# Eight modulation steps of the second layer, moved from the first layer's mixer to the end of its experts

## The chip, the cores and the metric

The kernel runs on one core of one Trainium2 chip, as one program. The metric is the device time of one execution, in microseconds (us). Four engines compute: TensorE (PE, with its weight loads listed as PEld), VectorE (DVE), ScalarE (ACT) and GpSimd (POOL). SyncE (SP) issues most transfers. Each engine works through its own instructions in order and waits at semaphores for the others.

## The reference, cut to what matters

The model is a backbone of two layers over 256 latent tokens and 256 context tokens of width 1024. Each layer is modulated by vectors that depend on the conditioning alone:

```python
for layer in range(DEPTH):
    m_lat = jnp.split((s_lat @ ada_w[layer] + ada_b[layer])[:, None, :], 6, axis=-1)
    m_ctx = jnp.split(s_ctx @ ada_w[layer] + ada_b[layer], 6, axis=-1)
    h = modulate(rms_norm(x, norm_mix_g[layer]), m_lat[0], m_lat[1])
    ...
    y, yc = token_mix(h @ w_in[layer], hc @ w_in[layer], ...)
    x = x + m_lat[2] * (y @ w_out[layer])
    h2 = modulate(rms_norm(x, norm_ffn_g[layer]), m_lat[3], m_lat[4])
    x = x + m_lat[5] * moe_ffn(h2, ...)   # 16 experts, two per token
```

The matrix `ada_w[layer]` has 1024 rows and 6144 columns in fp32, 24 MB for each layer. The kernel multiplies it with the two conditioning vectors. The last 2048 columns of the second layer (its chunks 4 and 5) are first used in that layer's mixture of experts.

## The kernel before, in words

**Stages.** Each layer has a mixer (the projection w_in in chunks, and four groups of attention, C, B, A, D), an output projection, the routing, and sixteen experts. A layer's weights pass through the on-chip memory once, in pieces of 1 MB.

**The stream of weights.** All weight loads are listed beforehand in `jobs`, in the order of their use. `pump` (line 127) takes the next job when a slot of 8 KB per partition is free and issues the load on SyncE; each load is kept behind the one before it. `next_w` hands the next loaded piece to the code and `done_w` gives its slot back. The first layer has three slots "a" that live through the whole kernel, and nine slots "b" that exist from the end of attention to the end of the experts. Jobs whose name begins with e or o (experts, output projection) may use every slot; the others (`in...`, `blk...`, `ada...`) only an "a" slot. A job that finds no slot it may use holds back all jobs behind it.

**The modulation.** Five groups of 2048 columns (two of layer 0, three of layer 1) are computed in forty steps by `ada_step` (line 307), eight steps to a group. A step takes one load of 1 MB and issues four matmuls of 32 columns by 512 rows, each on its own quarter of the array. The eighth step of a group also adds the bias (line 323), writes the rows to the DRAM tile `amd`, transposes them (line 330) and copies them to `modT` (line 333). In the kernel before, `Mixer.project` calls all forty steps in the first layer's mixer, between the products of the projection; `ADAN` says how many belong to each of the ten chunks of w_in.

**The order of instructions.** A scheduler orders each engine's instructions, by program order as priority and by when it takes them to be ready. `pinned` ties an instruction to the one traced before it on the same engine. The experts' matmuls are pinned, so TensorE runs them in the order of the code.

**The seam between the layers.** `Moe.experts` runs the first projection of expert e+1 (`first`, lines 1018 and 1023) ahead of the second projection of expert e (`second`, lines 1071 and 1077). `store` scales a result and scatters its rows to the DRAM tile `yd` with GpSimd (line 987). `overflow` (line 1136) follows the last expert: it loads the largest count of tokens on an expert (line 1140) and processes the tokens over capacity in a conditional (line 1141). The conditional is one unit to the scheduler, with work for all engines; here the count is under the capacity and it is passed over. Then the second layer begins: `combine` reads `yd` back (`yy`, on the same stream as the weights) and adds the rows to X (line 1220), `make_hT` normalises and transposes X (lines 406 to 436), and `split_w` (lines 456 and 458) splits the weights of the projection into two parts. The tiles of the second layer's beginning lie where the "b" slots and the experts' tiles were.

Of the kernel before, what the change touches and what calls it, by code (L numbers as in the profile page):

```python
# [44 lines left out]
GROUPS = ("C", "B", "A", "D")  # L45
CHUNKS = dict(A=("Aq", "Akv"), B=("Bq", "Bk", "Bv"), C=("Cq", "Ck", "Cv"), D=("Dq", "Dkv"))

ADAN = (0, 3, 5, 5, 4, 4, 5, 5, 4, 5)
CH = dict(Aq=0, Akv=256, Bq=512, Bk=768, Bv=1024, Cq=1280, Ck=1536, Cv=1792, Dq=2048, Dkv=2304)
YC = dict(A=0, B=2, C=4, D=6)  # L50

# [1 line left out]
def body(tc, a, dbg=None):  # L53
    nc = tc.nc
    ctx = ExitStack()
    V, S, G, PE = nc.vector, nc.scalar, nc.gpsimd, nc.tensor

    def pool(name, bufs=1, space=None, stack=None, side=None):
        kw = {} if space is None else dict(space=space)
        if side is not None:  # L60
            kw["side"] = side
        return (stack or ctx).enter_context(tc.tile_pool(name=name, bufs=bufs, reuse_waits="tile", **kw))
# [9 lines left out]
    def psum(tag):  # L72
        return ps.tile([128, 512], F32, name=tag, bufs=dict(mm=2, ada=1, tr=2, S=2, o=1)[tag])
# [20 lines left out]
    slots_free = []  # L94
# [7 lines left out]
    def add_ring(pl, tag, order):  # L102
        rings[tag] = pl
        for i in range(len(order)):
            pl.tile([128, 2048], F32, name=f"w{tag}{i}", bufs=1)
        slots_free.extend((tag, i) for i in order)
        pump()


    def add_tile(tag, t):  # L110
        fixed[tag, 0] = t
        slots_free.append((tag, 0))
        pump()

    def slot(x):
        return fixed[x] if x in fixed else rings[x[0]].tile([128, 2048], F32, name=f"w{x[0]}{x[1]}", bufs=1)

    def drop_ring(tag):
        assert all(x[0] != tag for x in used)
        slots_free[:] = [x for x in slots_free if x[0] != tag]  # L120


    def stream(out, in_):
        with tc.issue_after(state["dma"]) if state["dma"] is not None else nullcontext():
            state["dma"] = nc.sync.dma_start(out, in_).ins

    def pump():
        while slots_free and state["emit"] < len(jobs):
            nm, view, src = jobs[state["emit"]]
            xs = [y for y in slots_free if y[0] == "a" or nm[0] in "eo"]  # L130
            if not xs:
                break
            x = xs[0]
            slots_free.remove(x)
            t = slot(x)
            tv = t.rearrange("p (k n) -> p k n", n=view)
            stream(tv, src.rearrange("(k p) n -> p k n", p=128))
            issued.append((nm, x, tv))
            state["emit"] += 1

    def next_w(nm):
        if not issued:
            pump()
        n, tag, t = issued.pop(0)
        assert n == nm, (n, nm)
        used.append(tag)
        return t


    def done_w(n=1):  # L150
        for _ in range(n):
            slots_free.append(used.pop(0))
        pump()
# [3 lines left out]
    def jobs_ada(n):  # L157
        for _ in range(n):
            l, cg, k = ada_q.pop(0)
            jobs.append((f"ada{l}{cg}", 2048, a["ada_w"][l, 128 * k:128 * k + 128, 2048 * cg:2048 * cg + 2048]))  # L160
# [6 lines left out]
    order = [nm for g in GROUPS for nm in CHUNKS[g]]  # L167

    def job_in(l, nm):
        jobs.append((f"in{l}{nm}", 256, a["w_in"][l, :, CH[nm]:CH[nm] + 256]))  # L170

    for l in range(L):
        if l == 0:
            job_in(0, order[0])
            for j in range(4):
                for h in range(2):
                    c0 = 1024 * h + 256 * j
                    jobs.append((f"blk{j}", 256, a["ada_w"][0, :, c0:c0 + 256]))
        for i, nm in enumerate(order):
            if l or i:  # L180
                job_in(l, nm)
            if l == 0:
                jobs_ada(ADAN[i])
        for g in GROUPS:
            c0 = 128 * YC[g]
            jobs.append((f"out{l}{g}", 1024, a["w_out"][l, c0:c0 + 256]))

        for e in range(NE + 1):
            for hk in range(2):
                for nm in ("w_gate", "w_up"):  # L190
                    if e < NE:
                        jobs.append((f"e{l}", 512, a[nm][l, e, 512 * hk:512 * hk + 512]))
            for hk in range(2):
                if e:
                    jobs.append((f"e{l}", 1024, a["w_down"][l, e - 1, 256 * hk:256 * hk + 256]))


    pk = const.tile([128, PKN], F32, name="pk")
# [13 lines left out]
    sc, rwp = scr2[:, 0], scr2[:, 1]  # L212
# [91 lines left out]
    amd = dram.tile([32, 512], F32, name="amd")  # L304
    acur = {}

    def ada_step(scr):
        l, cg, k = ada_run.pop(0)
        if k == 0:
            acur["p"] = psum("ada")  # L310
            ab = acur["b"] = scr.tile([128, 512], F32, name="abr")
            G.memset(ab, 0.0)
            for s in range(2):
                nc.scalar.dma_start(ab[s:128:32], a["ada_b"][l, 2048 * cg:2048 * cg + 2048].rearrange("(c n) -> c n", c=4))
        pa, ab = acur["p"], acur["b"]
        w = next_w(f"ada{l}{cg}")
        for c in range(4):
            PE.matmul(pa[32 * c:32 * c + 32], lhsT=sc[:, k], rhs=w[:, 0, 512 * c:512 * c + 512],  # L318
                      start=k == 0, stop=k == 7)
        done_w()  # L320
        if k < 7:
            return
        V.tensor_add(ab, pa, ab)
        if cg:
            for s in range(2):
                r0 = ((l * 2 + cg - 1) * 2 + s) * 4
                nc.scalar.dma_start(amd[r0:r0 + 4], ab[s:128:32])
        pt = psum("tr").rearrange("p (q n) -> p q n", n=128)
        for q in range(4):
            PE.transpose(pt[:, q], ab[:, 128 * q:128 * q + 128], ident)  # L330
        c0, c1, d0 = ((0, 4, 0), (2, 4, 16), (0, 2, 24))[cg]
        for s in range(2):
            V.tensor_copy(modT[l][:, s, d0:d0 + 4 * (c1 - c0)].rearrange("p (c q) -> p c q", q=4),
                          pt[:, :, 32 * c0 + s:32 * c1:32].rearrange("p q c -> p c q"))
# [115 lines left out]
    def split_w(nm, pl, tag, bufs):  # L450
        w = next_w(nm)
        wp = []
        for q in range(4):
            x = pl.tile([128, 2, 2, 256], F32R, name=tag, bufs=bufs)
            r = w[:, 2 * q:2 * q + 2]
            S.activation(x[:, 0], r, AF.Copy)  # L456
            cnt["lo"] += 1
            (G if cnt["lo"] % 4 == 0 else V).tensor_sub(x[:, 1], r, x[:, 0].bitcast(F32))  # L458
            wp.append(x)
        done_w()  # L460
        return wp
# [55 lines left out]
    class Mixer:  # L517
# [7 lines left out]
        def project(self, nm, tiles, done):  # L525
            l = self.l
            begun = self.begun.pop(nm, None)
            if begun is None:
                with prefer(l, -70, 0):
                    wp = split_w(f"in{l}{nm}", self.ws, "ws", 5)  # L530
            n = ADAN[order.index(nm)] if l == 0 else 0
            for i, t in enumerate(tiles):
                if begun is None:
                    acc = psum_x("mm", l, 3)[:, 0:256]
                    products(acc, self.hT, wp, t, range(8))
                else:
                    acc = begun[t]
                self.flush()
                later = done(t, acc)
                if later is not None:  # L540
                    self.pending.append(later)
                for _ in range(n * (i + 1) // len(tiles) - n * i // len(tiles)):
                    ada_step(self.ada)
# [238 lines left out]
    class Moe:  # L782
        order = staticmethod(pinned)
# [674 lines left out]
    for l in range(L):  # L1458
# [50 lines left out]
        scr = pool(f"op{l}", stack=stR, side=P)  # L1509
# [5 lines left out]
        moe = (Moe if l < L - 1 else MoeOnChip)(l, tiles, pers, scr)  # L1515
# [5 lines left out]
        w = {k: next_w(f"out{l}{k}") for k in GROUPS[:-1]}  # L1521
# [3 lines left out]
        w = {g: next_w(f"out{l}{g}")}  # L1525
# [28 lines left out]
        with ExitStack() as stE:  # L1554
            moe.experts(pool(f"moee{l}", stack=stE, side=P))
            if l < L - 1:
                moe.overflow()
        drop_ring("c")
        drop_ring("b")
# [118 lines left out]
```

## Time and profile before

| | |
|---|---|
| time, median of 3 runs | 1228.39 us (1226.92 to 1229.65) |
| the profiled execution, its own time | 1229.94 us |
| its span in the profile | 1228.2 us |
| mean granted clock of TensorE | 0.963 |
| busy: TensorE, VectorE, ScalarE, GpSimd | 1122.8, 568.9, 417.5, 244.5 us |
| HBM read | 305.11 MB, 257 GB/s over the span |

Times in the rows are microseconds from the start of the span, or lengths in microseconds unless marked ns. L318 is line 318 of the kernel. Of a group or a piece of the timeline, "out<-in" names the tile written and the tile read, "x16" says that it stands for sixteen instructions, and the bracket at the end gives the idle time of the engine before it and what ended it. SPq, PEldq and the like are the sequencers of the engines: branches, register loads and semaphore instructions, and the issue of transfers. A matmul of fp32 appears as two records.

### The profile page before, as it was taken

The page shows a single profiled execution, that of the slowest core. Times are in us where ns is not written, and L with a number is a line of the kernel's source. Part 1 is how long each engine was busy: PE and PEld are TensorE (multiplying, and loading weights), DVE is VectorE, ACT ScalarE, POOL GpSimd, SP SyncE. Part 2 cuts the span into 40 slices and gives each one's busy share as a digit, 9 for nine tenths or more (in the row PEclk, how much of TensorE's full clock was granted, in tenths as well). Part 3 has the DMA queues.
Part 4 walks back from the last instruction along what each step waited for, and adds up shares of the span by engine and source line. Part 5 has one row for each costly group of instructions (what it writes and reads, how often), then busy time and mean ns, then how long its engine had stood idle before and what let it go on. Part 6 is the DMA issues. An engine that isn't in the chain of part 4 may idle for free. (4 is left out here: it accounts for less than half of the span.)

```text
span 1228.2 us, 21412 instructions
## 1 busy us (share of the span) xinstructions
PE 1122.8 (91%) x8495; PEld 653.6 (53%) x8495; DVE 568.9 (46%) x1544; ACT 417.5 (34%) x1003; POOL 244.5 (20%) x269
## 2 busy tenths in 40 slices
PE   4999999999999949999999993899999969999996
PEld 2677667676645424444444432888787533443432
DVE  4465666656433563232222216966775342333323
ACT  3345455446314311111111113675664221221212
POOL 1141221121111531122112113623231120000000
PEclk9899899999999969999999996998999989999999
DMA  9756455283570839999999957221424969999996
GB/s 305 240 185 241 173 172 194 101 292 140 204 279 18 325 125 314 377 383 381 375 367 379 378 219 265 78 70 35 129 70 161 355 260 393 393 394 394 394 394 244
DMA packets 134640, 313.00 MB, mean 255 GB/s; under 512 B 7212, under 2 KB 38448, under 8 KB 129408
## 3 DMA queue, kind: packets, MB, share of 16 engines
q1 hardware_dynamic: 127936, 294.19, 66.1%
q0 software_dynamic: 3840, 8.40, 2.1%
q10 hardware_dynamic: 2752, 8.91, 2.0%
q8 instruction: 71, 1.16, 0.4%
q14 instruction: 41, 0.34, 0.1%
HBM read 305.11 MB, written 10.55 MB: 257 GB/s over the span
## 5 line engine op out<-in xcount | busy, mean ns | idle before, releaser
L469 PE MATMUL mm<-ws,hT 128*128 128x256 f32 x1488 | 230.2, 296 | 3.6 <-DVE hT L508 1.8
L469 PEld LDWEIGHTS mm<-ws,hT 128*128 128x128 f32 x1488 | 201.0, 195 | 41.2 <-issue 25.1
L1018 PE MATMUL mm<-wb,xT 128*32 128x512 f32 x912 | 121.8, 622 | 0.0
L299 POOL TENSOR_TENSOR hss<-hss,mhalf 128x4 f32<-128x4 f32 (+2 forms) x56 | 67.6, 1210 | 184.9 <-DVE hss L298 176.5
L675 ACT ACTIVATE p<-S,nm 128x512 f32<-128x512 f32 (+1 forms) x120 | 73.7, 616 | 67.7 <-DVE nm L665 41.3
L665 DVE TENSOR_REDUCE nm<-S 128x1 f32<-128x512 f32 (+1 forms) x120 | 70.5, 596 | 25.8 <-PE S L640 21.8
L987 POOL DMA_INDIRECT yd<-y,idx x32 | 37.7, 1179 | 170.4 <-DVE y L1096 165.5
L769 PE MATMUL mm<-wa,t4k 128*128 128x512 f32 x144 | 70.8, 614 | 0.0
L1018 PE MATMUL mm<-wb,xTb 128*64 128x512 f32 x240 | 63.2, 596 | 0.8 <-DMA wb<-in_w_up_dram 0.8
L318 PE MATMUL ada<-wa,sc 128*32 128x512 f32 x320 | 63.1, 617 | 0.0
L1018 PEld LDWEIGHTS mm<-wb,xT 128*32 128x32 f32 x912 | 31.7, 114 | 55.6 <-issue 49.7
L1071 PE MATMUL S<-wb,hT 128*32 128x512 f32 (+1 forms) x360 | 56.1, 593 | 0.0
L648 PE MATMUL tr<-ident,p 128*128 128x128 f32 x320 | 51.0, 277 | 4.1 <-ACT p L675 3.5
L716 PE MATMUL o<-PT,v 128*64 128x256 f32 x320 | 54.5, 390 | 0.1
L456 ACT ACTIVATE ws<-wa 128x512 fp32r<-128x512 f32 x80 | 48.8, 630 | 16.9 <-PE mm L469 7.5
L458 POOL TENSOR_TENSOR ws<-wa,ws 128x512 fp32r<-128x512 f32 x20 | 27.9, 1395 | 133.3 <-ACT ws L456 108.5
L615 PE MATMUL tr<-identr,sk 128*128 128x128 f32 x312 | 47.5, 254 | 5.3 <-DVE sk L612 3.4
L1018 PE MATMUL mm<-wc,xTb 128*64 128x512 f32 x144 | 50.6, 596 | 0.0
L1057 ACT ACTIVATE hT<-tr 128x384 f32<-128x384 f32 (+1 forms) x32 | 14.0, 438 | 105.6 <-PE tr L1054 68.2
L648 PEld LDWEIGHTS tr<-ident,p 128*128 128x128 f32 x320 | 36.5, 140 | 22.5 <-ACT p L675 11.0
L458 DVE TENSOR_TENSOR ws<-wa,ws 128x512 fp32r<-128x512 f32 x60 | 43.5, 738 | 8.2 <-ACT ws L456 8.0
L615 PEld LDWEIGHTS tr<-identr,sk 128*128 128x128 f32 x312 | 35.0, 144 | 18.3 <-issue 7.4
(329 smaller groups left out, 1914.5 us busy)
## 6 DMA issues: line engine op xcount, KB each, us to landing
wb<-in_w_up_dram SPq DMA_DIRECT2D x49, 1024.0 KB
wa<-in_ada_w_dram SPq DMA_DIRECT2D x48, 1024.0 KB
wb<-in_w_gate_dram SPq DMA_DIRECT2D x38, 1024.0 KB
wb<-in_w_down_dram SPq DMA_DIRECT2D x30, 1024.0 KB
wa<-in_w_down_dram SPq DMA_DIRECT2D x22, 1024.0 KB
wa<-in_w_in_dram SPq DMA_DIRECT2D x20, 1024.0 KB
wc<-in_w_gate_dram SPq DMA_DIRECT2D x11, 1024.0 KB
wa<-in_w_gate_dram SPq DMA_DIRECT2D x10, 1024.0 KB
```

Of the source, the lines that this page charges most:

```text
L299: state["pow"] = G.tensor_tensor(out, x, mhalf[:x.shape[0], :x.shape[1]], op=OP.pow).ins
L318: PE.matmul(pa[32 * c:32 * c + 32], lhsT=sc[:, k], rhs=w[:, 0, 512 * c:512 * c + 512], start=k == 0, stop=k == 7)
L458: (G if cnt["lo"] % 4 == 0 else V).tensor_sub(x[:, 1], r, x[:, 0].bitcast(F32))
L469: PE.matmul(acc, lhsT=lh[:, k, c], rhs=wp[k // 2][:, rh, k % 2], start=first and k == 0 and i == 0, stop=last and k == 7 and i == 2)
L615: PE.transpose(pt[:, i], sk[:, i], identr)
L648: PE.transpose(pt[:, i], p[:, k0 + 128 * i:k0 + 128 * i + 128], ident)
L665: V.tensor_reduce(nm[:, 0:1], s[:, k0:512], axis=AX.X, op=OP.min)
L675: S.activation(p[:, k0:512], s[:, k0:512], AF.Exp, bias=nm_, scale=scale, accum_out=z)
L716: PE.matmul(o[64 * c:64 * c + 64, 256 * j:256 * j + 256], lhsT=v[:, 2 * st + kc, vc:vc + 64], rhs=PTs[c][:, kc], start=kc == 0, stop=kc == ...
L769: PE.matmul(acc, lhsT=self.yT[key][:, t // 2, i, 128 * (t % 2):128 * (t % 2) + 128], rhs=w[key][:, i, 512 * h:512 * h + 512], start=n == 0 ...
L1018: self.order(PE.matmul(pa[m * c:m * c + m], lhsT=xT[:, 4 * hk + k, m * t:m * t + m], rhs=w[m * c // 64][:, k], start=hk == 0 and k == 0, s ...
L1071: self.order(PE.matmul(py[m * c:m * c + m], lhsT=hT[:, f, m * t:m * t + m], rhs=wd[:, g, h:h + 512], start=f == 0, stop=f == 3))
```

## The change

The last eight steps, the group of the second layer's last 2048 columns (`ada12`), leave the first layer's mixer. `ADAN` is lowered from forty to thirty-two. Their loads are listed behind the first layer's experts and before the second layer's projection, and `pump` lets them use "b" slots only. The steps are called after the last expert and before the overflow path, with their matmuls pinned behind the last expert's; their bias tile comes from the experts' pool.

```diff
-ADAN = (0, 3, 5, 5, 4, 4, 5, 5, 4, 5)
+ADAN = (0, 3, 4, 4, 3, 4, 4, 3, 3, 4)
+LATE = ("ada12",)
...
-            xs = [y for y in slots_free if y[0] == "a" or nm[0] in "eo"]
+            xs = [y for y in slots_free if (y[0] == "b" if nm in LATE else y[0] == "a" or nm[0] in "eo")]
...
                     jobs.append((f"e{l}", 1024, a["w_down"][l, e - 1, 256 * hk:256 * hk + 256]))
+        if l == 0:
+            jobs_ada(8)
...
-    def ada_step(scr):
+    def ada_step(scr, order=lambda ins: None):
...
         for c in range(4):
-            PE.matmul(pa[32 * c:32 * c + 32], lhsT=sc[:, k], rhs=w[:, 0, 512 * c:512 * c + 512],
-                      start=k == 0, stop=k == 7)
+            order(PE.matmul(pa[32 * c:32 * c + 32], lhsT=sc[:, k], rhs=w[:, 0, 512 * c:512 * c + 512],
+                            start=k == 0, stop=k == 7))
...
             moe.experts(pool(f"moee{l}", stack=stE, side=P))
             if l < L - 1:
+
+                for _ in range(8):
+                    ada_step(moe.p2, pinned)
                 moe.overflow()
```

## Rows read from the trace of the kernel before

**Rows 1.** The page, its 40 slices: busy tenths of TensorE.

```profile
PE   4999999999999949999999993899999969999996
```

**Rows 2.** Busy time by stretch: first layer's mixer, second layer's mixer.

```profile
core 0: us, PE busy (x) PEld busy (x) DVE busy (x) ACT busy (x) POOL busy (x), PEclk, DMA share, GB/s
50.00:340.00 290.00, 281.80 (x1942) 198.29 (x1942) 179.08 (x558) 140.27 (x394) 67.60 (x87) 0.98 0.54 191
767.50:951.70 184.20, 172.87 (x1267) 148.68 (x1267) 133.66 (x370) 110.74 (x280) 62.05 (x69) 0.98 0.27 90
```

**Rows 3.** Waits of TensorE, 50 to 340 us: total, times, longest; the first of seven.

```profile
PE S L743 <- DVE zr L735: 2.3, 2, 1.4
```

**Rows 4.** The modulation in the mixer: its group of matmuls, and pieces of TensorE's timeline.

```profile
L318 PE MATMUL ada<-wa,sc 128*32 128x512 f32 x320 | 63.1, 617 | 0.0
...
100.25 1.92 PE L318 MATMUL ada<-wa,sc 128*32 128x512 f32 x16
...
103.58 0.66 PE L330 MATMUL tr<-ident,abr 128*128 128x128 f32 x4
```

**Rows 5.** Timeline of TensorE: experts 14 and 15, and where their slots are read.

```profile
709.19 1.91 PE L1023 MATMUL ada<-wb,xT 128*32 128x256 f32 x32
...
725.32 1.91 PE L1023 MATMUL o<-wb,xT 128*32 128x256 f32 x32
...
727.05 1.90 PE L1071 MATMUL S<-wa,hT 128*32 128x512 f32 x16
...
737.87 1.05 PE L1077 MATMUL S<-wb,hT 128*32 128x256 f32 x16
```

**Rows 6.** Timelines of ScalarE, VectorE and TensorE across the seam.

```profile
738.99 2.19 ACT L456 ACTIVATE ws<-wa 128x512 fp32r<-128x512 f32 x4 [3.32 <-PE S L1077]
...
749.15 3.92 DVE L1220 SCALAR_TENSOR_TENSOR x<-yy,wts,x 128x1024 f32<-128x1024 f32 x3 [7.25 <-DMA yy<-yd]
...
754.77 0.66 PE L429 MATMUL tr<-ident,xn 128*128 128x128 f32 x2 [15.85 <-DVE xn L418]
```

**Rows 7.** Timeline of SyncE at the seam: issues, merged (start, length, what).

```profile
729.87 6.89 SPq L125 DMA_DIRECT2D wa<-in_w_in_dram  x3
745.11 1.77 SPq L125 DMA_DIRECT2D yy<-yd  x4
```

**Rows 8.** The addition of the bias, line 323, on VectorE (ns min/median/max).

```profile
L323 DVE TENSOR_TENSOR abr<-ada,abr x5: 680/691/692, 102.2 to 331.4; 128x512 f32<-128x512 f32 x5
```

**Rows 9.** Busy time by stretch around the seam; the last two columns are DMA.

```profile
704.00:712.00 8.00, 7.84 (x94) 3.67 (x94) 1.67 (x3) 1.94 (x4) 0.00 (x0) 1.00 1.03 402
...
718.50:729.90 11.40, 11.40 (x150) 4.90 (x146) 1.30 (x3) 1.46 (x3) 0.64 (x1) 1.00 0.05 18
729.90:742.50 12.60, 8.38 (x102) 3.21 (x94) 4.72 (x8) 3.31 (x6) 5.04 (x8) 1.00 0.90 297
...
745.10:765.00 19.90, 5.28 (x23) 4.49 (x23) 12.27 (x16) 6.18 (x12) 2.84 (x4) 0.50 0.91 313
```

**Rows 10.** Sequencers at the conditionals: ns min/median/max, first and last start (us).

```profile
L1140 PEldq TENSOR_LOAD <-mxi x1: 488/488/488, 737.0 to 737.0; - x1
...
L1141 SPq EVENT_SEMAPHORE  x8: 17/17/17, 743.0 to 743.6; - x8
...
L1141 PEldq COMPARE_BRANCH  x1: 5548/5548/5548, 737.6 to 737.6; - x1
L1141 ACTq COMPARE_BRANCH  x1: 54/54/54, 740.0 to 740.0; - x1
...
L1141 POOLq INC_SWDGE_SEM  x1: 1144/1144/1144, 743.9 to 743.9; - x1
...
L1404 PEldq COMPARE_BRANCH  x1: 3742/3742/3742, 1220.4 to 1220.4; - x1
```

**Rows 11.** The scatters, line 987: GpSimd's instructions (ns), and their landing.

```profile
L987 POOL DMA_INDIRECT yd<-y,idx x32: 971/1004/1439, 487.1 to 740.4; - x32
...
DMA to landing us min/median/max: 3.4/6.2/7.0
```

## The prediction

> **What bounds the kernel now.** I read the forty slices of the page first, then busy time by stretch, then the waits of TensorE, and last the seam between the two layers, engine by engine. The slices show TensorE at nine tenths or more nearly everywhere, with two deep dips: one after the first layer's attention (where the routing is computed) and one at the seam, 738 to 760 us [rows 1]. The change takes work out of the first layer's mixer and puts it into the second dip, so two stretches decide.
>
> In the mixer, 50 to 340 us, TensorE is busy 281.80 of 290 us while VectorE is busy 179, ScalarE 140 and the DMA engines 0.54 of the time [rows 2]. It idles 8.2 us, 2.8%, and the longest entry of its waits there is 2.3 us in total [rows 3]. So a microsecond of TensorE work that leaves this stretch shortens the kernel by nearly a microsecond, up to what the waits give back. The modulation's steps are a fifth of that work: 320 recorded matmuls (40 steps, eight records each), 63.1 us busy, none with idle time ahead of it [rows 4].
>
> At the seam nothing bounds by throughput; it is a chain. TensorE ends the last expert at 738.9 [rows 5] and starts again at 754.77, idle 15.85 us [rows 6]. Between lie the last expert's scatter, the conditional of the overflow path (the `tc.If` at line 1141, not taken here), the reads of yd, and the combination. SyncE issues the first of these reads at 745.11 [rows 7], and VectorE has the data at 749.15 [rows 6].
>
> **Part one: the mixer loses eight steps.** At the mean of the row, 63.1 / 40 = 1.58 us, eight steps are 12.6 us. One group of four transposes goes with them, 0.66 us, so 13.3 us of TensorE work leaves. Where two steps run without a break they take 1.92 us, 0.96 each [rows 4]. From below, eight steps at 0.96 and the transposes make 8.3. I take the mean, because the steps that remain are scattered through the same code as now.
>
> The steps are also what TensorE does while others catch up. The second layer's mixer has none of them, and there it is busy 172.87 of 184.2 us, idle 6.2% [rows 2]. A fifth of the steps goes, so I let a fifth of the difference return: (6.2% - 2.8%) x 290 x 0.2 = 1.9 us. The mixer gains 13.3 - 1.9 = 11.4 us; bounds 8.3 and 13.3, and 3.7 if the whole difference comes back (a rival below). The group's addition (0.69 us of VectorE [rows 8]) and its copies leave engines that are not the bound. Eight loads of 1 MB leave a stretch whose DMA share is 0.54. The stages after the mixer start 11.4 us earlier with the same order of work.
>
> **Part two: the loads at the seam.** The last twelve jobs of the first layer are the last part of expert 14's first projection, down 13, expert 15's four pieces, down 14 and down 15. Three of these sit in the "a" slots: TensorE reads "wb" in all of them except down 14 and the first half of down 15, and the three loads of the next projection go out from 729.87 on, as those free [rows 5, 7]. So eight of the nine "b" slots come free before, between 711.1 (end of expert 14's first projection) and 727.2 (end of expert 15's) [rows 5], and the eight new loads can go out in that time, ahead of the next projection's. The rule in `pump` therefore holds no "a" slot back.
>
> Now the DMA engines. They are idle from 718.5 to 729.9 (share 0.05, 18 GB/s), with the old loads all landed; at full load they move 402 GB/s, 2.6 us per MB-load [rows 9]. Eleven loads in a row from about 718 make 28.7 us, and two experts' scatters (0.39 MB each, as their tiles say) 2.0 us: the last lands at about 748.7, where it now lands by 742.5 [rows 9]. The eighth new load lands near 739, when TensorE is done with the last expert: no step waits long.
>
> **Part three: the eight steps on TensorE, and the conditional behind them.** Pinned behind the last expert, eight steps run without a break. Two such steps take 1.92 us [rows 4], of which I take 0.2 for the tail of the last record, so one more step is 0.86 and eight are 7.1: TensorE works from 738.9 to 746.0 instead of idling. By itself this is hidden in the idle 15.85 us.
>
> What is not hidden is the queue. The conditional is one unit for all engines: each loads the count, branches, and passes a semaphore. TensorE's branch is the long one: 5548 ns, against 54 on ScalarE, and 3742 ns at the second conditional of the kernel, at its end [rows 10]. Today its sequencer comes there 1.9 us ahead of the engine (its load at 737.0, last matmul ending 738.9), passes at 743.2, and the chain waits for something else: GpSimd's last semaphore instruction, 743.9 to 745.05, which follows the last scatter's landing (issued at 740.4, landing 3.4 us later at best [rows 10, 11]). The read at 745.11 follows at once. With the steps ahead of it on its queue, TensorE branches later:
>
> If only the matmuls stand before the conditional, the load moves to 746.0 - 1.9 = 744.1, the branch to 744.7, and 5.55 us later it is 750.3: the read goes out at 750.4, 5.3 late. If the group's addition and transposes stand there too, the addition ends 0.69 after the matmuls [rows 8], the branch starts at 747.5, and the read goes at 753.2, 8.1 late. The trace of before can't tell which; I take the middle, 6.7. The other engines are no later: SyncE's eight semaphore waits at this line (743.0 to 743.6 now, where DMA traffic ends) would end near 749.0, from which a floor of 3.9 follows; a scatter that lands under load takes 6.2 us in the median [rows 11], so GpSimd passes at about 740.4 + 6.2 + 1.2 = 747.8.
>
> The splits of the next weights (ScalarE 2.19 us for four, waiting for TensorE's last read today [rows 6]) and the rope products on GpSimd lie in memory that the "b" slots leave, so they wait for steps now, until 746 at the latest; they are covered by the wait for the reads. If that cover is gone, they cost 2.2 us of ScalarE (a rival below). The memset and the two bias loads of the group are off the chain. Behind the read everything of the second layer shifts by the same amount; TensorE restarts at the lower of its levels in both cases (granted 0.50, which is 1.2 GHz, from 745.1 to 765 [rows 9]).
>
> The Trainium skill's page "Advanced Engine Details and Errata", section "Control Flow Timing", gives a compare-and-branch about 108 ns. By it TensorE would not be the last to pass, and the reads would go at the DMA floor. The rows above speak against it for TensorE alone. The page "Runtime: NRT & Kernel Launch" of the Trainium skill, section "Instruction fetch mechanics", says that a taken branch out of the fetched window stalls for a fetch, and the two long branches agree with that.
>
> **Sum.** -11.4 + 6.7 = -4.7 us. Against the profiled execution's own 1229.94 that is 1225.2; that execution was 1.55 us above the median of the runs, so against 1228.39 it is 1223.7.
>
> **The rivals.**
> B, the conditional is ahead of the steps in TensorE's queue, or its branch is quick. Then only the DMA floor of 3.9 counts: -7.5, 1220.9. For it: work of the second layer stands ahead of the conditional today, so the order is not that of the code. Against it: the steps are pinned to the last expert and come earlier in the code.
> C, the fillers are missed. TensorE's idle share in the first mixer rises to that of the second: 9.6 us come back, the mixer gives 3.7, and with 6.7 lost the kernel is 3.0 slower: 1231.4. It is slower at all once the mixer gives less than 6.7. For it: VectorE chains at the ends of attention already hold TensorE (line 743) [rows 3]. Against it: four fifths of the steps stay.
> D, everything of the group stands before the conditional and the splits stand in front of the statistics on ScalarE: 8.1 + 2.2 = 10.3 lost, -1.1: 1227.3. For it: the splits wait for the slots' last reader today [rows 6]. Against it: VectorE waits 7.25 us for the reads [rows 6], and ScalarE longer.
> Beside these, the granted clock over the mixer is 0.98 [rows 2], so stretches at the lower level cost it some 6 us now; half of that may come or go as the order changes.
>
> **How the numbers follow.** Forecast 0.52, B 0.18, D 0.18, C 0.12. The forecast's own range is 1220.4 to 1228.2 (mixer 13.3 with seam 5.3, mixer 8.3 with seam 8.1). About 0.2%, 2.5 us, is what a measurement of this kernel can tell from no change. Faster: 0.40 of the forecast, all of B, 0.02 of D, 0.60. Same: 0.12 of the forecast, 0.13 of D, 0.02 of C, 0.27. Slower: 0.10 of C and 0.03 of D, 0.13. The range reaches up into C and down to B with a full mixer and a clock stretch gained: 1216.5 to 1231.
>
> **What would show it.** Right: eight steps in the profile right after the last expert without gaps; TensorE's branch at line 1141 starting between 744 and 748 on the old time base (all of it some 11 us earlier) and lasting 4 to 6 us; the first yd read 5 to 8 us later, counted from the end of the last expert; DMA share near 1 where it is 0.05; the mixer 10 to 12 us shorter with idle near 10 us. Wrong: a mixer that shortens by less than 7 us, a read that goes out before TensorE passes the conditional, or steps that wait for their loads.

## The result, and the profile after

The changed kernel takes 1234.97 us (median of 8 runs, 1232.74 to 1241.18), the kernel before 1228.14 (8 runs): ratio 1.006, 95% interval [1.0041, 1.0078]. It is slower by 6.8 us, where 4.7 us less was forecast and 1231 was the upper end of the range. The profiled execution took 1235.47 us (span 1233.7), so the two traces differ by 5.5 us.

Marks in the two traces, in us from the start of the span (the starts and ends of TensorE's instructions):

| mark | before | after | shift |
|---|---|---|---|
| last projection product of the first mixer | 328.6 | 328.2 | -0.4 |
| output projection's unbroken run starts (all steps of the mixer done) | 338.2 | 337.2 | -1.0 |
| first product of the first layer's experts | 452.7 | 448.3 | -4.4 |
| last expert ends | 738.9 | 731.3 | -7.6 |
| first transpose of the second layer | 754.8 | 756.6 | +1.8 |
| end | 1228.2 | 1233.7 | +5.5 |

So the seam grows from 15.9 to 25.3 us, 9.4 more, and the first layer returns less than forecast. Of its 7.6 us, 1.0 is there at the end of the mixer, 3.4 come up to the experts, and 3.2 in the experts themselves, where nothing was changed (286.2 us before, 281.4 to 283.7 in all the other traces here). From the first transpose to the end the traces differ by another 3.7 us; in the kernels below this stretch is 473 to 478 us long without following the edits, so I read it as the spread of single executions.

**The mixer.** Busy time by stretch, after (compare [rows 2]):

```profile
50.00:340.00 290.00, 278.92 (x1875) 196.81 (x1874) 178.13 (x556) 139.57 (x394) 67.03 (x87) 0.99 0.48 164
```

The waits of TensorE there (waiter, releaser, total, times, longest), before (these come next to the one in [rows 3]) and after:

```profile
PE S L743 <- DVE zr L740: 2.0, 3, 0.8
PE mm L469 <- DVE hT L508: 1.8, 1, 1.8
PE tr L615 <- DVE sk L612: 0.7, 1, 0.7
```

```profile
PE S L746 <- DVE zr L743: 2.3, 4, 0.9
PE tr L618 <- DVE sk L615: 1.9, 1, 1.9
PE S L746 <- DVE zr L738: 1.9, 2, 1.0
PE mm L472 <- DVE hT L511: 1.8, 1, 1.8
PE S L643 <- ACT st L450: 1.0, 1, 1.0
PE o L719 <- DVE PT L448: 0.8, 1, 0.8
```

TensorE's busy time falls by 2.88 us, and its idle time rises by as much, from 8.2 to 11.1. The three longest waits of before are still there; one of 0.7 us has grown to 1.9, and smaller ones have come. The group of the modulation's matmuls, after (compare [rows 4]):

```profile
L321 PE MATMUL ada<-wa,sc 128*32 128x512 f32 x256 | 60.3, 610 | 0.0
```

Sixty-four of 320 records left, a fifth, but only 2.8 of 63.1 us. The reason is visible in TensorE's timeline of the changed kernel (start, length, line, count):

```profile
105.91 1.05 PE L321 MATMUL ada<-wa,sc 128*32 128x512 f32 x2
106.89 0.50 PE L643 MATMUL S<-st 128*128 128x512 f32 x1
107.32 1.06 PE L321 MATMUL ada<-wa,sc 128*32 128x512 f32 x6
108.31 1.21 PE L472 MATMUL mm<-ws,hT 128*128 128x256 f32 x8
...
114.31 1.06 PE L321 MATMUL ada<-wa,sc 128*32 128x512 f32 x8
```

Two records take 1.05 us, six and eight take 1.06. A step's four matmuls write four different quarters of the PSUM partitions (32 rows each), two records for each, and by these times they run side by side. What costs is a *piece*, an unbroken run of such records, about 1.05 us whatever is in it up to one step; a second step in the same piece adds 0.86 (1.92 less 1.06), and a step that is torn in two costs twice. Before, the 40 steps lay in 54 pieces (19 of them of two records, five that reach into a second step); after, 32 steps lie in 56 pieces (26 of two records, one that reaches into a second step). At these prices that is 61.0 us before and 59.7 after; most of the rest of 63.1 and 60.3 is in pieces of one step or less that took longer (two of 1.9 us, one of 1.5).

**The seam.** TensorE's timeline, after (compare [rows 5, 6]):

```profile
730.27 1.05 PE L1080 MATMUL S<-wb,hT 128*32 128x256 f32 x16
731.13 7.05 PE L321 MATMUL ada<-wb,sc 128*32 128x512 f32 x64
739.06 0.66 PE L333 MATMUL tr<-ident,abr 128*128 128x128 f32 x4 [0.87 <-DVE abr L326]
756.62 0.66 PE L432 MATMUL tr<-ident,xn 128*128 128x128 f32 x2 [16.91 <-DVE xn L421]
```

SyncE's issues in the changed kernel, merged (compare [rows 7]):

```profile
703.52 16.94 SPq L126 DMA_DIRECT2D wb<-in_ada_w_dram  x8
722.27 14.63 SPq L126 DMA_DIRECT2D wa<-in_w_in_dram  x3
746.09 2.65 SPq L126 DMA_DIRECT2D yy<-yd  x4
```

The sequencers at its conditional, now line 1144 (compare [rows 10]; ns min/median/max, first and last start in us):

```profile
L1144 SPq EVENT_SEMAPHORE  x8: 17/17/17, 741.9 to 745.6; - x8
...
L1144 POOLq INC_SWDGE_SEM  x1: 1144/1144/1144, 738.6 to 738.6; - x1
L1144 PEldq COMPARE_BRANCH  x1: 5937/5937/5937, 739.7 to 739.7; - x1
...
L1144 PEldq EVENT_SEMAPHORE  x1: 51/51/51, 745.7 to 745.7; - x1
```

The same line on SyncE, 743 to 746 us alone:

```profile
L1144 SPq EVENT_SEMAPHORE  x6: 17/17/17, 745.3 to 745.6; - x6
```

The eight steps run without a gap. The first read of yd goes out 14.8 us after the last expert's end, before 6.2: 8.6 us later, and from the read to the first transpose there are 10.5 us, before 9.7. Two things end together in front of the read. TensorE comes to its branch only behind the group's transposes and leaves it at 745.6. SyncE's eight semaphore instructions are waits for eight groups of transfers (so the program has it: on the skipped path of the `tc.If` SyncE waits for the transfers under way); the third belongs to the last load of the next projection and passes at 745.3. GpSimd, the last before, is through at 739.7. The DMA engines, 722 to 746 us in 40 slices of 0.6 us, show how that load ends:

```profile
DMA  9999999999999999989898999888999852210000
GB/s 382 396 410 410 410 437 423 423 427 434 420 372 396 420 376 369 340 309 345 295 278 282 358 386 386 280 273 299 367 372 369 278 172 91 94 55 22 20 0 0
```

Full until about 741, then a tail that falls from 172 to 20 GB/s and ends at 744.8. The third load of the projection left SyncE at 736.9, 5.6 us after the last expert's end; before, the same load was out at 736.8, 2.1 us ahead of it [rows 7].

### The profile page after: what moved, and what is told of

Read it like the earlier page. It is cut to its first block, busy times and chain, and to the rows that moved or that the text cites. A ratio compares the mean times of both kernels' runs of the same rounds, so it can differ in the third digit from the quotient of the medians.

```text
span 1233.7 us, 21433 instructions
## 1 busy us (share of the span) xinstructions
PE 1126.1 (91%) x8495; PEld 658.0 (53%) x8495; DVE 569.3 (46%) x1544; ACT 416.4 (34%) x1003; POOL 243.8 (20%) x269
## 5 line engine op out<-in xcount | busy, mean ns | idle before, releaser
L1021 PE MATMUL mm<-wb,xT 128*32 128x512 f32 x912 | 118.7, 606 | 0.0
L1021 PE MATMUL mm<-wb,xTb 128*64 128x512 f32 x240 | 63.1, 596 | 0.8 <-DMA wb<-in_w_up_dram 0.8
L321 PE MATMUL ada<-wa,sc 128*32 128x512 f32 x256 | 60.3, 610 | 0.0
L461 DVE TENSOR_TENSOR ws<-wa,ws 128x512 fp32r<-128x512 f32 x60 | 44.2, 749 | 11.7 <-ACT ws L459 11.5
```

Source lines behind the costliest of these rows:

```text
L321: order(PE.matmul(pa[32 * c:32 * c + 32], lhsT=sc[:, k], rhs=w[:, 0, 512 * c:512 * c + 512], start=k == 0, stop=k == 7))
L1021: self.order(PE.matmul(pa[m * c:m * c + m], lhsT=xT[:, 4 * hk + k, m * t:m * t + m], rhs=w[m * c // 64][:, k], start=hk == 0 and k == 0, s ...
```

## The experiments

Each was measured beside the kernel before, which had medians of 1228.5 to 1228.9 us there. The ratios are to that kernel, with their 95% intervals.

**Pieces or missing fillers.** Two theories of why the mixer gave nothing. P: the cost goes with the pieces, and the change left their number as it was. F: the steps filled TensorE's waits, and the waits came back. To tell them apart, the second to fourth matmul of a step are kept right behind the first, in the kernel before (`glue_before`) and in the changed one (`glue_after`):

```diff
 # glue_after
-            order(PE.matmul(pa[32 * c:32 * c + 32], lhsT=sc[:, k], rhs=w[:, 0, 512 * c:512 * c + 512],
-                            start=k == 0, stop=k == 7))
+            with tc.high_priority(3000) if c else nullcontext():
+                mm = PE.matmul(pa[32 * c:32 * c + 32], lhsT=sc[:, k], rhs=w[:, 0, 512 * c:512 * c + 512],
+                               start=k == 0, stop=k == 7)
+            if c:
+                pinned(mm)
...
```

> The kernel before with one edit: the second to fourth matmul of a modulation step are tied to the one ahead of them and given a high priority, so that TensorE runs the four of a step together. Theory P (pieces): a run of one step's records costs about 1.0 us on TensorE whether it holds one, two, three or all four of the matmuls, because the four work side by side; the mixer of before has its 40 steps in 54 such runs, the edit leaves 38. It should save 16 x 1.0 us, of which 2 to 4 come back as waits: 1212 to 1216 us. Theory F (fillers): the changed kernel's mixer did not shorten because waits came back where the steps had filled them; the number of runs does not matter, and tied steps fill worse: 1228 to 1233 us.

> The changed kernel with the same edit. P: its 32 steps in the mixer stand in 56 runs, the edit leaves 32; 24 us less on TensorE, 3 to 5 back as waits, from 1235: 1214 to 1218 us, so not below the kernel before with the edit, since the seam still loses 8 to 9 us. F: no change, about 1235 us.

Measured: `glue_before` 1216.81 us, ratio 0.9903 [0.9876, 0.9929]; `glue_after` 1215.38, ratio 0.9898 [0.9874, 0.9922]. The pieces fall from 54 to 38 and from 56 to 32, and the group with them. The group in the mixer, of `glue_before` and then of `glue_after`:

```profile
L319 PE MATMUL ada<-wa,sc 128*32 128x512 f32 x320 | 42.8, 613 | 0.0
```

```profile
L322 PE MATMUL ada<-wa,sc 128*32 128x512 f32 x256 | 35.0, 619 | 0.0
```

The same 320 records cost 63.1 us in 54 pieces and 42.8 in 38. P holds; under F, with no step taken away, nothing would have been won. Of the 20.3 us, 11.8 reach the kernel's time; `glue_before` stays 0.8 above the range expected under P.

**The two parts alone.** `mixer_only` has the change's mixer with 32 steps; the last group is left out (steps, loads, sum), and other values stand in its place. `seam_only` has the mixer of before with its 40 steps and computes the last group a second time behind the last expert:

```diff
 # mixer_only
...
+    V.memset(modT[1][:, :, 24:32], 0.5)
...
-                for _ in range(8):
-                    ada_step(moe.p2, pinned)
 # seam_only
...
-    ada_run = list(ada_q)
+    ada_run = list(ada_q) + [(1, 2, k) for k in range(8)]
...
```

> The changed kernel without the last group: thirty-two steps in the mixer with the changed ADAN, nothing at the seam; the group's loads and matmuls are left out and its results are replaced by other values. P: the mixer has 56 runs of steps against 54 in before, so it ends within 1 us of before; up to the experts 4 us less as in the changed kernel's profile, seam as before: 1223 to 1228 us. The forecast's mixer (11.4 us less) would give 1217. F: waits eat most of it, 1221 to 1226, with TensorE's idle time in the mixer up by 8 us or more.

> The kernel before with all forty steps in its mixer, and the last group computed once more at the seam, with its eight loads in b slots, as the change does. It has the seam's cost without the mixer's saving. In the changed kernel the first read of yd goes out 14.8 us after the last expert's end against 6.2. P and F alike: mixer as before, seam 8 to 9 us longer, 1236 to 1238 us. If the second layer loses time on its own account, as the profile of the changed kernel hints (2.0 us in its mixer, 1.5 behind it), 1239 to 1241.

Measured: `mixer_only` 1227.44 us (12 runs, 1221.69 to 1234.08), ratio 0.9998 [0.9981, 1.0016], 56 pieces. `seam_only` 1238.83, ratio 1.0077 [1.0054, 1.0101], seam 26.3 us. So the seam alone costs some 10 us, and the mixer's part alone is worth nothing that these runs can tell, at most 2.3 us. In the trace of `mixer_only` TensorE idles 9.1 us between 50 and 340, 0.9 more than before, where F asked for 8 more. The changed kernel is 3.9 us below `seam_only`, with intervals that overlap; the mixer's share is thus 0 to 4 us. The profiled execution of `mixer_only` was the fastest of the twelve, 5.8 us under their median: a single trace, that of the changed kernel with its 7.6 us included, can't size the gain to better than this.

**What a piece costs, by itself.** `half_cols` is `glue_before` with only two of a step's four matmuls in seven steps of eight; half of the modulation's columns therefore hold one product of eight.

```diff
...
-        for c in range(4):
+        for c in range(4 if k == 0 else 2):
...
```

> The kernel before with each step kept in one run (glue_before, 1216.8 us, 38 pieces, 41.9 us of the group in the first layer's mixer), and in seven steps of eight only two of the step's four matmuls left, so half of the modulation's columns hold one product of eight. Theory P (a piece costs about 1.0 us whether one or four column quarters are in it): the number of pieces stays, the group's time in the mixer stays within 2 us of 41.9 though 140 of its 320 records are gone, time 1215 to 1218. Rival (cost goes with the records, as the forecast counted): 140 of 320 records fewer, the group falls to 24 us and the time to about 1199.

Measured: 1221.01 us (1214.53 to 1222.65), ratio 0.9913 [0.9882, 0.9945]. The group in the mixer of `half_cols` (columns as in [rows 4]), and two pieces of its timeline:

```profile
L319 PE MATMUL ada<-wa,sc 128*32 128x512 f32 x180 | 42.6, 614 | 0.0
```

```profile
109.44 1.05 PE L319 MATMUL ada<-wa,sc 128*32 128x512 f32 x4
...
123.99 1.91 PE L319 MATMUL ada<-wa,sc 128*32 128x512 f32 x8
```

140 records fewer, and the group stays at 42.6 us (42.8 with all of them); a step of four records takes the 1.05 us of one of eight, and two such steps 1.91. P holds for the group, and the price by records (24 us) is refuted. The time missed the expected 1215 to 1218 on the far side; its interval overlaps that of `glue_before`, so nothing is read from that.

**Which wait holds the read of yd.** Two theories. S1: TensorE's late branch. S2: SyncE's wait for the transfers under way. All four kernels are `glue_after` with one or two edits at the seam. `g_one_load` serves all eight steps from one load (the group is computed from one slab of weights); `g_tail_behind` has the sum, transposes and copies written behind the overflow path, and the scheduler then puts 19 of the 32 matmuls behind the conditional too; `g_one_load_tail_behind` is both; `g_loads_only` keeps the eight loads and leaves out the steps and the sum, with other values in their place.

```diff
 # g_one_load
-            jobs_ada(8)
+            jobs_ada(1)
...
 # g_tail_behind
...
+        if (l, cg) == (1, 2):
+            acur["tail"] = lambda: ada_tail(l, cg, pa, ab)
...
                 moe.overflow()
+                acur["tail"]()
 # g_loads_only
...
-                    ada_step(moe.p2, pinned)
+                    next_w("ada12")
+                    done_w()
```

> The kernel after with each mixer step kept in one run (glue_after, 1215.4 us), and at the seam one 1 MB load serves all eight steps, so seven of the eight loads are gone; the last modulation group is therefore computed from one slab of weights, not eight. Theory S1 (TensorE reaches its branch only after the 32 matmuls and the tail, 739.1 us in the kernel after, stays in it 5.9 us, and the read of the layer's sums waits for that): the seam does not get shorter, 26 to 27 us from the last expert's end to the layer's first transpose, time 1214 to 1217. Rival S2 (SyncE stands ahead of the conditional for the landing of the transfers in flight, the last load of the next projection at 741.1 to 741.5 us): seven megabytes less at some 0.40 MB per us land up to 17 us earlier, so the read goes 3 to 4 us earlier, time 1211 to 1212.

> glue_after with the group's sum, four transposes and copies written behind the conditional; in the program 13 of the 32 seam matmuls stay ahead of TensorE's branch, 19 and the tail come behind it. S1: TensorE branches some 5 us earlier (19 of 32 matmuls at 7.05 us for all is 4.2, the tail's wait 1.0), the read goes as much earlier, and what is behind the branch runs beside the read's flight: seam 19 to 21 us, time 1208 to 1210. S2: the landing still holds the branch: 0 to 4 us less, 1211 to 1215.

> Both edits: one load for the eight seam steps (group computed from one slab of weights), and the tail with 19 of the matmuls behind the conditional. S1 and S2 both: the read goes 6 to 8 us earlier, time 1207 to 1209; under S1 this equals g_tail_behind within 1 us, under S2 it is 3 us or more below it.

> glue_after with the eight seam loads kept and the eight steps, the sum, the transposes and the copies left out; the group's values are replaced by others. S1: TensorE branches right behind the last expert, the seam is that of the kernel before, 16 to 17 us, time 1204 to 1207. S2: the landings still hold SyncE: seam 20 to 25 us, time 1210 to 1214.

Measured, in us (the last four columns counted from the last expert's end, in the profiled execution; "both" is `g_one_load_tail_behind`):

| kernel | median | ratio to before | TensorE out of its branch | SyncE's last wait | read of yd | first transpose |
|---|---|---|---|---|---|---|
| before | 1228.14 | | 4.3 | 4.7 | 6.2 | 15.9 |
| after | 1234.97 | 1.006 [1.0041, 1.0078] | 14.3 | 14.3 | 14.8 | 25.3 |
| `glue_after` | 1215.38 | 0.9898 [0.9874, 0.9922] | 13.5 | 14.5 | 15.2 | 26.7 |
| `g_one_load` | 1213.58 | 0.9884 [0.9860, 0.9907] | 11.9 | 10.4 | 12.1 | 22.9 |
| `g_tail_behind` | 1214.06 | 0.9890 [0.9871, 0.9910] | 6.5 | 10.0 | 11.9 | 25.5 |
| both | 1213.26 | 0.9878 [0.9856, 0.9899] | 6.1 | 4.8 | 7.5 | 23.2 |
| `g_loads_only` | 1221.07 | 0.9947 [0.9928, 0.9967] | 5.0 | 8.5 | 10.1 | 24.1 |

Neither theory holds alone. With seven of the loads gone, SyncE is past the projection's last load at 4.6; it then waits until 10.4 for the group's own rows, which ScalarE writes to `amd`, and TensorE's branch holds the read at 12.1 (S1). SyncE's last wait ahead of that read (the longest of these six, 1362 ns), and TensorE past its branch:

```profile
L126 SPq EVENT_SEMAPHORE  x6: 17/28/1362, 725.3 to 725.6; - x6
...
L1153 PEldq EVENT_SEMAPHORE  x1: 51/51/51, 726.8 to 726.8; - x1
```

With TensorE early (`g_tail_behind`), the landing holds the read, and behind it two of the projection's loads, which now leave between the conditional and the read, at 11.9 (S2). With both out of the way the read goes at 7.5, nearly where it went before, and as before right behind GpSimd's last semaphore instruction (7.4; before 6.1). The transpose still comes 23.2 us after the expert. Of the four times only that of `g_tail_behind` lies in a range that was expected (S2's); "both" was expected at 1207 to 1209 under either theory, because the queue that is left behind the read was not foreseen. Where that time goes is in the timelines of TensorE (one line) and VectorE in `g_one_load_tail_behind` (expert's end 714.2, read 721.70):

```profile
720.57 5.96 PE L325 MATMUL ada<-wb,sc 128*32 128x512 f32 x38 [2.93 <-PEq L1159]
...
726.64 0.69 DVE L341 TENSOR_TENSOR abr<-ada,abr 128x512 f32<-128x512 f32 x1 [11.92 <-DMA yy<-yd]
727.25 1.28 DVE L476 TENSOR_TENSOR ws<-wa,ws 128x512 fp32r<-128x512 f32 x2
728.45 0.23 DVE L351 COPY modT<-tr 128x8 f32<-128x8 f32 x2
729.64 0.69 DVE L476 TENSOR_TENSOR ws<-wa,ws 128x512 fp32r<-128x512 f32 x1 [0.96 <-ACT ws L474]
730.68 1.34 DVE L476 TENSOR_TENSOR ws<-wa,ws 128x512 fp32r<-128x512 f32 x1 [0.34 <-ACT ws L474]
731.94 3.79 DVE L1238 SCALAR_TENSOR_TENSOR x<-yy,wts,x 128x1024 f32<-128x1024 f32 x3
```

The group's sum waits on VectorE for the steps behind the branch, the splits of the next weights stand behind it, and the combination behind those: a queue of the kind of rival D, on VectorE. In `g_loads_only` no step runs at all, and the seam is 24.1 us: the landing, then the two loads that leave ahead of the read. VectorE has the data 8.4 us after the read's issue, 4.0 in the kernel before; it is done with its last split at 735.1 and waits 3.29 us more for them (same columns):

```profile
734.42 0.69 DVE L468 TENSOR_TENSOR ws<-wa,ws 128x512 fp32r<-128x512 f32 x1 [3.95 <-ACT ws L466]
738.40 3.80 DVE L1230 SCALAR_TENSOR_TENSOR x<-yy,wts,x 128x1024 f32<-128x1024 f32 x3 [3.29 <-DMA yy<-yd]
```

That kernel's time is above `glue_after`'s, which neither theory gave. In the two traces the output projection starts at the same time (308.6), and the first expert 7.8 us later than in `glue_after`; what holds it up in between was not tried, so only the seam is read here.

**A version that beats both.** `glue_before`, `glue_after` and `g_tail_behind` compute everything, and each is about 1% below the kernel before (12 to 14 us) and 18 to 21 us below the changed one. Among the three the intervals overlap, so whether the eight steps are better late or early is not settled once they are in one piece each: late saves 7.8 us of the group in the mixer (42.8 to 35.0) and costs some 10 us at the seam. In the two single traces the last projection product comes 6.2 us earlier with the late steps (305.9 against 312.1) and the first expert 11.5 (429.0 against 440.5), so with whole steps the mixer's part of the change is worth several microseconds.

## Why the prediction was wrong

**The step that failed.** "At the mean of the row, 63.1 / 40 = 1.58 us, eight steps are 12.6 us." The mean was taken as a price for each step. The cost went with the pieces, 1.05 us each, 54 of them for 40 steps, and the number of pieces is set by where the scheduler tears steps apart, not by the number of steps. With 32 steps it tore more of them (56 pieces), and the group lost 2.8 us where 12.6 were counted; even these come from fewer pieces with a second step and fewer slow ones, while the number of pieces rose by two. The sentence behind the choice, that "the steps that remain are scattered through the same code as now", was the assumption that did not hold. The row itself held the warning: 0.96 us for a step in a run against 1.58 in the mean [rows 4]; I used the 0.96 as the lower bound of the removal (8.3), when even that supposed that a whole step leaves with its pieces.

**The returned waits.** Forecast 1.9 us; TensorE's idle time in the stretch rose by 2.9. This is 1.0 more than forecast, and it stands against 2.8 us of matmuls and 0.66 of transposes, not against 13.3. So the mixer's end moved by 1.0 us in the trace (2.8 in that of `mixer_only`), where 11.4 was forecast; up to the last expert's end the one trace shows 7.6, the medians 0 to 4. The forecast had the stages behind the mixer start earlier "with the same order of work". In the traces they gave something of their own: ahead of one transpose in the attention that follows (L648, waiting for ScalarE's `p`) TensorE idles 2.00 us before and 1.96 in `seam_only`, 0.58 after and not at all in `mixer_only`.

**The seam.** Forecast 5.3 to 8.1 us, middle 6.7; the read went 8.6 later, the seam grew by 9.4. The eight steps took 7.05 us (forecast 7.1), and all of the group stood ahead of the branch, the upper case (8.1). The cause given was half of it: TensorE's branch (5937 ns) and the last landing ended within half a microsecond, and in SyncE's order the landing was the last to be waited for, 745.3. My floor for the transfers, 3.9, was too low: it took the eleven loads as one run at full rate. The run was as counted (it was to end 9.8 us after the last expert, and the DMA engines are full until 9.9 after it); left out was the tail of 3.6 us behind it, for which SyncE waits too.

**The rivals.** B (branch quick or ahead of the steps) fell: TensorE's branch took 3588 to 6329 ns in all seven seams of the table. The Trainium skill's page "Advanced Engine Details and Errata", section "Control Flow Timing", gives about 108 ns for a compare-and-branch; ScalarE's 54 and VectorE's 72 ns here are of that order, TensorE's are not, and the measurement decides. C had the sign (slower by 3.0; measured 6.8), with the wrong mechanism: of the 9.6 us of idle time that it had come back, 2.9 did, and `glue_after` has the same 32 steps and fewer pieces and is 19.6 us faster than the changed kernel. D's splits set nothing in the changed kernel (VectorE was done with them at 745.4 and waited 4.53 us for the reads), but they are what comes next once the read is early. Of the signs named beforehand, "a mixer that shortens by less than 7 us" is the one that came; the eight steps without gaps and the branch of 5.9 us came as forecast.

## What to carry to other kernels

Before a mean is used as the price of a removed instruction, look in the timeline at what one instance costs in each of its surroundings; where matmuls on different quarters of the array run side by side, count unbroken runs, and keep the partners together before moving them. Work put into an idle stretch is free only if nothing that ends the stretch queues behind it: here a branch on its engine, a wait for the transfers under way at a conditional, and the next engine's queue each held the chain at almost the same time, and taking one away showed the next. A single trace sizes no gain below the spread of the runs.

## What the runs showed of the hardware that was not expected

A run of two, four, six or eight records of the 32-column matmuls mostly took 1.05 to 1.07 us in the timeline, and halving the matmuls of a step changed its time by nothing (1.05). TensorE's branch over the skipped path took 5548 ns before, 5937 after, and between 3588 and 6329 in the kernels of the table, over the same skipped code; what sets its length was not tried. The last load before the conditional ended at some 20 GB/s around 744 us, where 410 were moved twenty microseconds earlier. Its packets are not slower there: from 743 to 744.8 us 43 of them take 6.9% of the time of 16 engines, 46 ns each, and from 738 to 740.5 us 844 take 100.7%, 48 ns each. The share is that of about one engine that still has work; why the work ends unevenly was not tried.
